# Attention's bulk transfers moved to ScalarE's queue, and a ninth pair of query tiles computed ahead, in a two-layer decoder trunk

## The chip, the core and the metric

The kernel runs on one core of one Trainium2 chip. The metric is device time in microseconds of one execution of the whole program. The kernel before takes 1128.87 us, the median of 3 runs (1127.96 to 1128.97). TensorE is called PE below, VectorE DVE, ScalarE ACT, GpSimd POOL and SyncE SP, as in the profile.

## What is computed

Layer A is a gated linear attention over 1024 tokens of width 1024 with its output projection and a layer norm; layer B, which the change touches, is the second layer:

```python
k, v = shared_kv(x, w_kv)                       # 3 groups x 2 heads x 128, rope on k
q, g = split(x @ w_in)                          # q: 3 groups x 8 heads x 128, rope; g: 8 x 128
for gi, (window, dilation) in enumerate(((128, 1), (512, 4), (2048, 16))):
    o_g, lse_g = dilated_window_attention(q[gi], k[gi], v[gi], window, dilation)
wts = softmax(stack(lses), axis=0)              # weights over the three groups
o = sum(wts * stack(outs))
x = layer_norm(ALPHA * x + (o * silu(g)) @ w_out)
```

All of it is float32. The large products are made of three PE products each (high part by high part, high by low, low by high) in the fast float32r format.

## The kernel before, in words

**Recording and order.** The kernel does not issue instructions itself. It records them with what they read and write into an object `S`, and the scheduler `Sched.order` (line 266) simulates the engines with a table of costs, gives each instruction a planned start, and issues all of them sorted by it. So an edit of one statement, or of a cost, can move instructions on every engine. All instructions therefore carry one source line in the profile (L465), and are told apart by the tiles that they write and read. Each engine then works through its own list strictly in that order; an instruction whose data are late holds up those behind it.

**Transfers.** A `dma_start` is itself an instruction of the engine that issues it: SP issues nearly all, POOL those that add to a tile in flight. The program counts the landing of SP's transfers on eight counters, DMAHW0 to DMAHW7, dealt out in turn in the order of the whole program; a transfer that gets a counter waits until the transfer that had this counter before it has landed. The scheduler's model has one time, `dma_free` (line 293), for all transfers in flight, and does not know the counters.

**Layer B.** It stands in `layer_b` (line 1212) and has three parts.

1. Values, then keys and some queries by pairs. `seven` (line 1295) computes two 1024x128 tiles at once with seven products of half tiles in place of eight (the Strassen-Winograd scheme): 7 products x 4 pieces of depth x 3 = 84 PE instructions of 128x512, tile `sev`. The list `jobs` has three pairs of key tiles, then the pairs of query tiles in `EARLY` (line 41), each entry being two heads and a group: eight pairs, which cover groups 1 and 2 of all eight heads. Results go through the tile `pair` to a DRAM tile `qd`.
2. Attention, one head u after the other (loop at line 1651). `q_proj(u)` (line 1442) gets the three query tiles of a head: those in `qd` are loaded (`Q<-qd`, 512 KB each), the others are computed by `project` (line 687): 2 halves x 8 pieces of depth x 3 = 48 PE instructions of 128x512, tile `acc`. `g_proj(u)` (line 1452) computes the head's gate with another 48. Both take their weights with `load_w` (line 653): a load `wf<-in_wB` of 512 KB, then on ACT the high part `wh<-wf` and a negated copy `wl<-wf`, to which POOL's adding transfer gives the low part. After a query projection ACT copies halves (`t<-acc`) and DVE and POOL rotate them; after a gate projection ACT makes a tanh (`th<-acc`) and DVE the rest (`sg`).
   `scores(u)` (line 1469) makes the score products `lv<-K,Q` on PE; DVE masks each into the tile `P`, with its minimum (`sts`, `nat`), which frees the PSUM bank, of which two are in use; ACT takes the exponential in place. The row statistics are then brought into another order through DRAM with many small transfers: `std<-sts`, `nat<-std`, `cwd<-ew`, `cw<-cwd`, 2 to 4 KB each, 18 per head. `attend(u)` (line 1555) scales P by these weights, transposes it (`ms`), and multiplies with V into two PSUM banks (`po`), from which `og<-po` copies the result. Heads 4 to 7 use a second set of keys and values, so that K and V are loaded again in the middle (`reload_k(1)`, `reload_v(1)`); gated results go to DRAM (`ogB<-og`).
3. The output projection (`ogh`, `ogl` with the weights `in_wOB`) and the layer norm.

All transfers named here are issued by SP but for POOL's adding ones, and land in one ring of SP's.

Of the kernel before, what the change touches and what calls it, by code (L numbers as in the profile page):

```python
# [37 lines left out]
OWN = {"PE": 0.0, "SP": 0.0, "DVE": 0.115, "ACT": 0.11, "POOL": 0.1}  # L38
RUNS, GATHER = 0.3, 1.0
QUEUED, ISSUE, ADDED = 2.4, 0.9, 1.7  # L40
EARLY = [(0, 1, 2), (2, 3, 2), (0, 1, 1), (2, 3, 1), (4, 5, 2), (6, 7, 2), (4, 5, 1), (6, 7, 1)]


class Buf:
# [100 lines left out]
class Sched:  # L145
# [120 lines left out]
    def order(self):  # L266
# [3 lines left out]
        free = {e: 0.0 for e in self.ENG}  # L270
# [19 lines left out]
                for e in o.engs:  # L290
                    ready[e].append(o)
        done = []
        dma_free = 0.0
        cur_set = None
        INF = 1e18

# [32 lines left out]
        while n_done < len(ops):  # L329
            best = None  # L330
            for e in self.ENG:
                cand = None
                for o in ready[e]:
                    if o.t0 is not None:
                        continue
                    r = soft = o.least
                    for d in o.deps:
                        q = ops[d]
                        t = q.t1 + (OWN[e] * (d in o.raw) if q.eng == e else self.pad.get((q.eng, e), self.lat))
                        r = max(r, t)  # L340
                        soft = max(soft, t + (AHEAD if e == "PE" and q.eng in ("ACT", "DVE", "POOL") else 0.0))
                    if o.first:
                        t = alloc_time(o)
                        r = max(r, t)
                        soft = max(soft, t + (AHEAD if e == "PE" and t > 0 else 0.0))
                    if r >= INF:
                        continue
                    k = o.engs.index(e)
                    st = max(free[e], r, port) if o.port[k] else max(free[e], r)
                    if any(max(free[q], r) <= st and c < o.cost[o.engs.index(e)] for q, c in zip(o.engs, o.cost)):  # L350
                        continue

                    key = (max(st, soft), o.prio)
                    if cand is None or key < cand[0]:
                        cand = (key, o, st)
                if cand is not None:
                    (late, pr), o, st = cand
                    if best is None or (late, pr) < best[0]:
                        best = ((late, pr), o, e, st)
            if best is None:  # L360
                left = [o for o in ops if o.t0 is None]
                raise RuntimeError(f"no instruction can be issued; {len(left)} left, first {left[0].calls[0][0]} "
                                   f"{[v.buf.name for v in left[0].writes]}")
            _, o, e, st = best
            c = o.cost[o.engs.index(e)]
            if o.func is not None and e == "ACT":
                new = act_set(o.func, cur_set)
                if new != cur_set:

                    c += 1.3 if cur_set else 0.0  # L370
                    cur_set = new
            o.t0, o.eng = st, e
            if o.calls[0][0] == "dma_start":
                added = e == "POOL"
                dma_free = max(dma_free, st + ISSUE * added) + c * (ADDED if added else 1.0)
                o.t1 = dma_free + (QUEUED if added else 1.7)
                free[e] = st + (ISSUE if added else 0.37)
            else:
                o.t1 = st + c
                free[e] = o.t1  # L380
                if o.port[o.engs.index(e)]:
                    port = o.t1
            for b in o.first:
                if b.placed:
                    continue
                b.placed = True
                tg = tags[id(b.pool), b.tag]
                tg["next"] += 1
                if len(tg["live"]) >= tg["bufs"]:
                    old = min((x for x in tg["live"] if all(u.t0 is not None for u in x.users)),  # L390
                              key=lambda x: max(u.t1 for u in x.users))
                    tg["live"].remove(old)
                tg["live"].append(b)
            for p in {id(v.buf.pool) for v in o.reads + o.writes}:
                pool_users[p]["left"] -= 1
                pool_users[p]["end"] = max(pool_users[p]["end"], o.t1)
            for q in o.engs:
                ready[q].remove(o)
            for s in o.succ:
                s.left -= 1  # L400
                if s.left == 0:
                    for q in s.engs:
                        ready[q].append(s)
            done.append(o)
            n_done += 1
# [216 lines left out]
def trunk(tc, xT, wP, wA, wA12, wAv3, w2, wO, wK, wV0, wV12, wB, wOB, par_d,  # L622
          ident_d, lmask_d, cos_d, sin_d, bmask_d, rmask_d, tri_d, lnr_d, out):
    S = Sched(tc, lat=LAT, pad=PAD)
# [25 lines left out]
        return slice(half * 512, half * 512 + 512)  # L650


    def load_w(src, added=False):
        with S.later(-WEIGHTS):
            return load_w_now(src, added)

    def load_w_now(src, added):
        k, c = src.shape[1], src.shape[2]
        wf = wts.tile([128, 1024], F32, name="wf", bufs=2)
        wf = wf[:, :k * c].rearrange("p (k c) -> p k c", k=k)  # L660
        S.sync.dma_start(wf, src)
        hi = wts.tile([128, 1024], FR, name="wh", bufs=3)
        hi = hi[:, :k * c].rearrange("p (k c) -> p k c", k=k)
        split_hi(hi, wf)
        lo = wts.tile([128, 1024], FR, name="wl", bufs=3)
        lo = lo[:, :k * c].rearrange("p (k c) -> p k c", k=k)
        if added:
            S.scalar.activation(lo, wf, AF.Copy, scale=-1.0)
            S.gpsimd.dma_start(lo, src, accum_op=OP.add)
        else:  # L670
            split_lo(lo, wf, hi)
        return hi, lo
# [515 lines left out]
    kd = [[dram.tile([128, T], F32, name=f"kd{c}{g}") for g in range(3)] for c in range(2)]  # L1188
    vd0 = [dram.tile([128, T], F32, name=f"vd0{c}") for c in range(2)]
# [22 lines left out]
    def layer_b(xs, early):  # L1212
# [27 lines left out]
        K = [[None] * 3 for _ in range(2)]  # L1240
# [139 lines left out]
        def load_v(c, g):  # L1380
            V[c][g] = page(p0, F32, f"V{c}{g}")
            if g == 1:
                for n in range(2):
                    S.sync.dma_start(
                        V[c][g].rearrange("p (r n e) -> p r n e", r=4, n=2)[:, :, n, :],
                        vd[n * 512:n * 512 + 512, c * 128:c * 128 + 128].rearrange("(p r) e -> p r e", r=4))
            else:

                src = vd3[c].rearrange("(n a s k j) e -> k s a n (j e)", n=8, a=8, s=2, k=2)
                for k in range(2):  # L1390
                    for s in range(2):
                        S.sync.dma_start(V[c][g][k * 64:k * 64 + 64, s * 512:s * 512 + 512], src[k, s])

        def sigmoid_gate(sg, acc):
            th = small("th", "t1", 2)
# [21 lines left out]
        def reload_k(c):  # L1417
            for g in (2, 1, 0):
                K[c][g] = page(p0, F32, f"K{c}{g}")
                S.sync.dma_start(K[c][g], kd[c][g])  # L1420

        def reload_v(c):
            load_v(c, 2)
            load_v(c, 1)
            V[c][0] = page(p0, F32, f"V{c}0")
            S.sync.dma_start(V[c][0], vd0[c])

        reload_k(0)

# [12 lines left out]
        def q_proj(u):  # L1442
            Q = [page(p0, F32, "Q") for _ in range(3)]
            U[u]["Q"] = Q
            for g in range(3):
                if (u, g) in qd:
                    S.sync.dma_start(Q[g], qd[u, g])
                else:
                    project(wB[u, g], xs, lambda half, acc: rope(Q[g], g, half, acc), added=u > 0)


        def g_proj(u):
            og = U[u]["og"]

            def evac(half, acc):
                sg, r = small("sg", "t2", 2), hs(half)
                sigmoid_gate(sg, acc)
                S.vector.scalar_tensor_tensor(og[:, r], og[:, r], 0.5, sg, op0=OP.mult, op1=OP.mult)
                if u < 6:
                    S.sync.dma_start(ogB[u][:, r], og[:, r])  # L1460
            project(wB[u, 3], xs, evac, added=True)

        def pieces(P, g, j0):
# [182 lines left out]
            S.vp.memset(x, 0.0)  # L1646
        q_proj(0)
        reload_v(0)
        scores(0)
        q_proj(1)  # L1650
        for u in range(7):
            if u == 3:
                with S.behind(cwd[3]):
                    reload_k(1)
            scores(u + 1)
            if 0 < u < 5:
                g_proj(u - 1)
            if u + 2 < 8:
                q_proj(u + 2)
            attend(u)  # L1660
            if u == 3:
                reload_v(1)
        for u in (4, 5, 6):
            g_proj(u)
        early()
# [185 lines left out]
```

## Time and profile before

| | |
|---|---|
| median of 3 runs | 1128.87 us |
| the profiled execution | 1128.91 us |
| its span, first to last instruction | 1127.1 us |
| granted TensorE clock, mean | 0.999 |
| busy share of the span | PE 99%, PE's weight loads 84%, DVE 73%, ACT 53%, POOL 19% |
| layer A and the values of layer B | 0 to 503 us |
| pairs (`sev`) | 503 to 713 us |
| attention, with the first output products | 713 to 1047 us |
| the rest | 1047 to 1127 us |

A row of the profile names engine, operation, output<-inputs, shape and count, then busy time and the mean duration of one. On PE a matmul of 128x512 stands there with some 390 ns, but the next one starts after 227 ns, because they overlap in the pipeline: a stage's PE time is its number of instructions times their spacing, not the sum of durations. Idle time in square brackets is the gap between the end of one instruction and the start of the next on the engine, with what ended it. On a queue (SPq) a duration is the time in which the sequencer was busy with issuing, not the transfer.

### The profile page before, as it was taken

To read this page: it belongs to the slowest core of one execution; us is meant where nothing else is said; L and a number is where in the kernel's file an instruction comes from. 1 tells how busy PE (TensorE), PEld (TensorE's weight loads), DVE (VectorE), ACT (ScalarE), POOL (GpSimd) and SP (SyncE) were. 2 spreads that over 40 slices of the span, in tenths; PEclk is the share of its full clock that TensorE was granted. 3 is DMA by queue.
4 is the path that set the end of the run, shared out by engine and by line. 5 is a ranking of instruction groups with operands and counts; after the bars stand their busy time and mean duration, and the time that the engine had idled before them with its cause. 6 is when DMAs were issued, how large, how long until landed. Compare 5 with 4: busy or idle time off the path is not lost.

```text
span 1127.1 us, 20068 instructions
## 1 busy us (share of the span) xinstructions
PE 1115.3 (99%) x7648; PEld 950.0 (84%) x7648; DVE 826.0 (73%) x1646; ACT 597.7 (53%) x1199; POOL 214.4 (19%) x209
## 2 busy tenths in 40 slices
PE   9999999999999999999999999999999999999997
PEld 9888888888988888998888888878888888888876
DVE  6286862687968489897888888567875767776578
ACT  5355542546464256666556656476664666643252
POOL 1000100112122031232223232322221123312010
PEclk9999999999999999999999999999999999999999
DMA  7211132221152444865656566955445553442644
GB/s 258 75 39 39 57 95 75 75 76 39 60 191 84 143 163 155 272 193 138 176 133 170 133 175 171 274 111 100 96 111 136 139 127 77 98 120 77 186 134 175
DMA packets 106768, 145.12 MB, mean 129 GB/s; under 512 B 45136, under 2 KB 63440, under 8 KB 106672
## 3 DMA queue, kind: packets, MB, share of 16 engines
q1 hardware_dynamic: 100192, 128.11, 36.5%
q0 software_dynamic: 6480, 15.73, 8.1%
q8 instruction: 60, 0.98, 0.4%
q14 instruction: 36, 0.29, 0.1%
HBM read 112.15 MB, written 31.65 MB: 128 GB/s over the span
## 4 chain that ended last, share of the span: by engine, by line
PE 91%; DVE 4%; DMA 2%; ACT 2%; issue 1%; POOL 0%; SPq 0%; DVEq 0%; ACTq 0%
PE acc L465 42%; PE sev L465 19%; PE po L465 9%; PE lv L465 8%; PE vac L465 7%; PE ms L465 4%; PE pro L465 2%; DMA wf<-in_wOB 1%; DVE P L465 1%; DVE rt L465 1%; DVE wl L465 1%; DVE t L465 0%; DMA xf<-in_xT 0%; DVE x1l L465 0%; ACT t L465 0%
## 5 line engine op out<-in xcount | busy, mean ns | idle before, releaser
L465 ACT ACTIVATE wh<-wf 128x1024 fp32r<-128x1024 f32 (+3 forms) x115 | 105.4, 919 | 159.9 <-PE acc L465 97.3
L465 PE MATMUL acc<-x1h,wh 128*128 128x512 f32 x256 | 114.0, 445 | 0.0
L465 PE MATMUL sev<-T,wh 128*128 128x512 f32 x352 | 108.3, 389 | 0.0
L465 DVE TENSOR_TENSOR wl<-wf,wh 128x1024 fp32r<-128x1024 f32 (+3 forms) x61 | 73.9, 1213 | 42.4 <-ACT wh L465 32.3
L465 PE MATMUL acc<-xh,wh 128*128 128x512 f32 x256 | 101.8, 398 | 0.0
L465 PE MATMUL acc<-x1h,wl 128*128 128x512 f32 x256 | 100.6, 393 | 0.0
L465 PE MATMUL acc<-x1l,wh 128*128 128x512 f32 x256 | 100.1, 391 | 0.0
L465 PE MATMUL acc<-xh,wl 128*128 128x512 f32 x256 | 99.8, 390 | 0.0
L465 PE MATMUL acc<-xl,wh 128*128 128x512 f32 x256 | 99.8, 390 | 0.0
L465 PEld LDWEIGHTS sev<-T,wh 128*128 128x128 f32 x352 | 66.1, 188 | 13.7
L465 ACT ACTIVATE P<-P,sts 128x256 f32<-128x256 f32 (+1 forms) x128 | 59.7, 468 | 30.5 <-DVE sts L465 28.4
L465 POOL DMA_DIRECT2D wl<-in_wB x39 | 34.6, 887 | 209.5 <-ACT wl L465 207.9
L465 PE MATMUL lv<-K,Q 128*64 128x64 f32 (+2 forms) x512 | 71.3, 288 | 1.8 <-DVE sts L465 1.8
L465 PE MATMUL sev<-T,wl 128*128 128x512 f32 x176 | 68.5, 389 | 0.0
L465 PEld LDWEIGHTS lv<-K,Q 128*128 128x128 f32 (+1 forms) x512 | 54.0, 163 | 14.9 <-DVE sts L465 4.4
L465 DVE CUSTOM_DVE_ANT_0 P<-lv,bmask 128x256 f32<-128x256 f32 (+1 forms) x128 | 46.4, 377 | 21.5 <-PE lv L465 21.0
L465 PE MATMUL acc<-ogh,wh 128*128 128x512 f32 x152 | 60.1, 396 | 0.1
L465 PE MATMUL acc<-ogl,wh 128*128 128x512 f32 x152 | 59.3, 390 | 0.0
L465 PE MATMUL acc<-ogh,wl 128*128 128x512 f32 x152 | 59.2, 390 | 0.0
L465 POOL TENSOR_TENSOR wl<-wf,wh 128x1024 fp32r<-128x1024 f32 x10 | 24.2, 2418 | 181.4 <-PE ms L465 91.5
L465 PEld LDWEIGHTS acc<-x1h,wl 128*128 128x128 f32 x256 | 48.0, 188 | 10.8
L465 PEld LDWEIGHTS acc<-xh,wl 128*128 128x128 f32 x256 | 48.1, 188 | 10.3
(304 smaller groups left out, 2997.3 us busy)
## 6 DMA issues: line engine op xcount, KB each, us to landing
wf<-in_wB SPq DMA_DIRECT2D x32, 512.0 KB
wf<-in_wA SPq DMA_DIRECT2D x24, 512.0 KB
wf<-in_wO SPq DMA_DIRECT2D x16, 512.0 KB
qd<-pair SPq DMA_DIRECT2D x16, 512.0 KB
Q<-qd SPq DMA_DIRECT2D x16, 512.0 KB
wf<-in_wOB SPq DMA_DIRECT2D x16, 512.0 KB
wl<-in_wB POOLq DMA_DIRECT2D x15, 512.0 KB, 7.8
wf<-in_wV SPq DMA_DIRECT2D x12, 512.0 KB
```

The lines of the kernel that those rows point to most:

```text
L465: getattr(handle[o.eng], meth)(*[conv(a) for a in args], **{k: conv(v) for k, v in kw.items()})
```

## The change

- `EARLY` gets a ninth pair, (3, 6, 0): group 0 of the heads 3 and 6. `q_proj(3)` and `q_proj(6)` load these two tiles; their two projections fall away.
- A variable `carrier` names the engine that issues the large transfers. It is SP, ACT from behind the first `q_proj(0)` and `reload_v(0)` until the loop over heads has been recorded, then SP again. It holds for weights (`wf`), keys, values, query tiles and gated results. The statistics' transfers always remain on SP.
- The scheduler's model gets one time per queue, and counts 0.6 us for the issue of a small transfer where it counted 0.37.

```diff
-EARLY = [(0, 1, 2), (2, 3, 2), (0, 1, 1), (2, 3, 1), (4, 5, 2), (6, 7, 2), (4, 5, 1), (6, 7, 1)]
+EARLY = [(0, 1, 2), (2, 3, 2), (0, 1, 1), (2, 3, 1), (4, 5, 2), (6, 7, 2), (4, 5, 1), (6, 7, 1),
+         (3, 6, 0)]
...
-        dma_free = 0.0
+        queues = {"SP": 0.0, "ACT": 0.0, "POOL": 0.0}
...
-                dma_free = max(dma_free, st + ISSUE * added) + c * (ADDED if added else 1.0)
-                o.t1 = dma_free + (QUEUED if added else 1.7)
-                free[e] = st + (ISSUE if added else 0.37)
+                line = "ACT" if e == "ACT" else "SP"
+                queues[line] = max(queues[line], st + ISSUE * added) + c * (ADDED if added else 1.0)
+                o.t1 = queues[line] + (QUEUED if added else 1.7)
+                small = max(int(_np.prod(v.shape)) for v in o.reads[:1] + o.writes[:1]) <= 2048
+                free[e] = st + (ISSUE if added else 0.6 if small else 0.37)
...
+    carrier = [S.sync]
+
...
-        S.sync.dma_start(wf, src)
+        carrier[0].dma_start(wf, src)
...
-                S.sync.dma_start(K[c][g], kd[c][g])
+                carrier[0].dma_start(K[c][g], kd[c][g])
...
-                    S.sync.dma_start(Q[g], qd[u, g])
+                    carrier[0].dma_start(Q[g], qd[u, g])
...
-                    S.sync.dma_start(ogB[u][:, r], og[:, r])
+                    carrier[0].dma_start(ogB[u][:, r], og[:, r])
...
         q_proj(0)
         reload_v(0)
+        carrier[0] = S.scalar
         scores(0)
...
             if u == 3:
                 reload_v(1)
+        carrier[0] = S.sync
         for u in (4, 5, 6):
```

The four transfers of `load_v` and the last one of `reload_v` are changed in the same way.

In the program as built, PE has 1008 instructions `sev` where it had 924, and 672 of 128x512 with x1 into `acc` where it had 768. ACT issues 43 transfers: 16 `Q`, 9 `wf`, 8 `ogB`, 7 `V` and 3 `K`. SP keeps those of head 0, the weights of the last four gates, and the statistics. Up to the eighth query pair every engine's list is unchanged.

**ACT, early in attention.** Before, the first heads' weights, query copies (`t`) and the exponentials of head 0 stand there like this:

```order
L465 ACTIVATE t_7128<-acc 64x512 x2
L465 ACTIVATE wh<-wf 128x1024
L465 ACTIVATE wl<-wf 128x1024
L465 ACTIVATE t_7188<-acc 64x512 x2
L465 ACTIVATE t_7217<-acc 64x512 x2
L465 ACTIVATE P,nat<-P,nat 128x64 x8
L465 ACTIVATE P,sts<-P,sts 128x128
```

The same place after the change:

```order
L468 ACTIVATE wh<-wf 128x1024
L468 ACTIVATE wl<-wf 128x1024
L468 DMA wf<-in_wB 128x1024
L468 ACTIVATE t_7363<-acc 64x512 x2
L468 ACTIVATE P,nat<-P,nat 128x64 x4
L468 ACTIVATE t_7420<-acc 64x512 x2
L468 ACTIVATE P,nat<-P,nat 128x64 x4
```

The load of the next weights now stands on ACT between the negated copy that frees its tile and the query copies that DVE waits for. In six of the nine such places a `t` or `th` stands right behind the load.

**SP before, ACT after, at the second set of values.** The rows are shown with what they wait for (DMAHW0 to DMAHW7 are the counters, the others engines; `std` and `nat` are statistics of head 4). Before, on SP:

```order
L465 DMA std_8745<-sts 128x2x4 [waits DMAHW3_49,Activation_49]
L465 DMA Q<-qd_6972 128x1024 [waits DMAHW4_49,PE_49]
L465 DMA Q<-qd_6644 128x1024 [waits DMAHW5_49]
L465 DMA V_8810<-vd_4625 64x1x512 [waits DMAHW6_49,PE_49]
L465 DMA V_8810<-vd_4625 64x1x512 [waits DMAHW7_49]
L465 DMA V_8824<-vd 128x4x128 [waits PE_49]
L465 DMA V_8847<-vd_4834 128x1024 [waits DMAHW1_49,PE_49]
L465 DMA std_8745<-sts 8x16x8 [waits DMAHW2_49,DVE_49]
```

After, on ACT:

```order
L468 DMA Q<-qd_6982 128x1024 [waits DMAHW0_49]
L468 DMA Q<-qd_6644 128x1024 [waits DMAHW4_49]
L468 DMA V_8933<-vd_4625 64x1x512 [waits DMAHW5_49,Pool_49]
L468 ACTIVATE P,sts<-P,sts 128x256 [waits DVE_49] x2
L468 DMA V_8933<-vd_4625 64x1x512 [waits DMAHW6_49]
L468 DMA V_8944<-vd 128x4x128 [waits DMAHW7_49,PE_49]
L468 DMA V_8951<-vd_4834 128x1024 [waits DMAHW0_49,PE_49]
L468 ACTIVATE og<-po 128x64x4 x2
L468 ACTIVATE P,sts<-P,sts 128x256 [waits DVE_49] x2
L468 DMA V_8933<-vd_4625 64x1x512 [waits DMAHW1_49]
```

Seven value transfers and two query loads now stand between ACT's exponentials and its copies out of the `po` banks. The counters are dealt out over both queues together, so `V_8951`, which gets DMAHW0 after `Q<-qd_6982`, waits on ACT until that load has landed.

More of the change, by code (lines that the diff above doesn't have):

```diff
@@ L1383, in load_v @@
                 for n in range(2):
-                    S.sync.dma_start(
+                    carrier[0].dma_start(
                         V[c][g].rearrange("p (r n e) -> p r n e", r=4, n=2)[:, :, n, :],
@@ L1391, in load_v @@
                     for s in range(2):
-                        S.sync.dma_start(V[c][g][k * 64:k * 64 + 64, s * 512:s * 512 + 512], src[k, s])
+                        carrier[0].dma_start(V[c][g][k * 64:k * 64 + 64, s * 512:s * 512 + 512], src[k, s])
         def sigmoid_gate(sg, acc):
@@ L1425, in reload_v @@
             V[c][0] = page(p0, F32, f"V{c}0")
-            S.sync.dma_start(V[c][0], vd0[c])
+            carrier[0].dma_start(V[c][0], vd0[c])
         reload_k(0)
```

## The prediction

> **What bounds the kernel now.** I read the page first, then busy time by stage, then the spacing of PE's instructions, then the places where PE sits idle in the stage that changes.
>
> ```profile
> span 1127.1 us, 20068 instructions
> PE 1115.3 (99%) x7648; PEld 950.0 (84%) x7648; DVE 826.0 (73%) x1646; ACT 597.7 (53%) x1199; POOL 214.4 (19%) x209
> ```
>
> ```profile
> core 0: us, PE busy (x) PEld busy (x) DVE busy (x) ACT busy (x) POOL busy (x), PEclk, DMA share, GB/s
> ...
> 503.30:712.76 209.46, 209.46 (x925) 173.42 (x925) 170.11 (x247) 126.87 (x218) 58.68 (x57) 1.00 0.61 162
> 712.76:1046.60 333.84, 332.05 (x2074) 286.45 (x2073) 235.11 (x776) 191.62 (x582) 78.30 (x103) 1.00 0.49 119
> ```
>
> The rows of the second view are the stage of the pairs and attention. PE is never idle in the first and idle for 333.84 - 332.05 = 1.79 us in the second, at the full granted clock (1.00). A busy PE need not be a PE at its pace, so I take the spacing from the chain of work that ended last, whose rows are start, time, instruction and count:
>
> ```profile
> 503.30 209.47 PE sev L465 x924
> 712.76 17.00 PE acc L465 x75
> ```
>
> 209.47 / 924 = 0.2267 us, and 17.00 / 75 = 0.2267 us: the products of the pairs and those of the ordinary projections cost PE the same, each 128x512, and the eleven pairs go through without a gap. So PE's list is the bound in both stages, and a change is worth what it takes off that list plus or minus what PE waits. The waits of attention are few. The timeline of PE shows them; the first two rows are how each looks, the others are the late instruction alone:
>
> ```profile
> 741.54 0.40 PE L465 MATMUL acc<-x1h,wl 128*128 128x512 f32 x1
> 742.30 0.38 PE L465 MATMUL lv<-K,Q 128*128 128x128 f32 x1 [0.37 <-DVE sts L465]
> ...
> 760.31 0.48 PE L465 MATMUL lv<-K,Q 128*128 128x256 f32 x1 [0.46 <-DVE sts L465]
> ...
> 796.01 0.38 PE L465 MATMUL lv<-K,Q 128*128 128x128 f32 x1 [0.20 <-DVE sts L465]
> ...
> 884.12 0.48 PE L465 MATMUL lv<-K,Q 128*128 128x256 f32 x1 [0.60 <-DVE sts L465]
> ...
> 979.81 0.48 PE L465 MATMUL lv<-K,Q 128*128 128x256 f32 x1 [0.15 <-DVE sts L465]
> ```
>
> Each is a score product that waits for a PSUM bank which DVE has yet to read. The gaps sum to 1.78 us, all of the stage's idle time. What is lost is a little more, since the product ahead lasts 0.40 us where the next would start after 0.23: 5 x 0.17 = 0.85 more, 2.6 us in all. That is the most that better timing in attention can bring, and no transfer stands as the releaser of any of the five.
>
> **The ninth pair.** Removed from attention are two projections of 2 x 8 x 3 = 48 PE instructions, 96 x 0.2267 = 21.76 us; added to the pairs are 7 x 4 x 3 = 84, 19.04 us. PE's list gets shorter by 12 x 0.2267 = **2.72 us**. The new pair's other work lies beside PE: by the stage's row a pair costs DVE 170.11 / 11 = 15.5 us, ACT 11.5 and POOL 5.3 against PE's 19.04. If that cover failed there would be a gap after a pair, and there is none in eleven. Its two stores and two loads of 512 KB are new, 2 MB in a stage whose transfer engines are busy for 0.61 and another with 0.49; I count them at nothing, and at 0.3 us at most, half of the largest gap above, should one delay a page.
>
> In attention the projections also leave the other engines:
>
> ```profile
> L465 ACT ACTIVATE wh<-wf 128x1024 fp32r<-128x1024 f32 x19 | 20.1, 1060 | 32.0 <-PE acc L465 23.2 <-PE lv L465 4.4 <-PE po L465 4.4
> L465 ACT ACTIVATE t<-acc 64x512 f32<-64x512 f32 x32 | 19.0, 593 | 12.7 <-DVE t L465 9.9 <-PE acc L465 2.5
> L465 ACT ACTIVATE wl<-wf 128x1024 fp32r<-128x1024 f32 x13 | 13.5, 1042 | 0.0
> ```
>
> ACT loses 2 x (1.06 + 1.04 + 4 x 0.593) = 8.9 us, so 191.6 becomes 182.7.
>
> **ACT as an issuer.** No trace here has ACT issuing a transfer; the nearest rows are those of the same transfers on SP (shortest, middle, longest ns on the queue):
>
> ```profile
> L465 SPq DMA_DIRECT2D Q<-qd x16: 377/440/974, 720.1 to 950.9; - x16
> L465 SPq DMA_DIRECT2D wf<-in_wB x32: 328/333/732, 536.0 to 922.2; - x32
> L465 SPq DMA_DIRECT2D V<-vd x14: 321/572/751, 721.3 to 891.8; - x14
> L465 SPq DMA_DIRECT2D ogB<-og x12: 320/325/1135, 788.8 to 999.5; - x12
> L465 SPq DMA_DIRECT2D K<-kd x6: 319/374/448, 697.2 to 860.5; - x6
> ```
>
> 16 x 0.440 + 9 x 0.333 + 7 x 0.572 + 8 x 0.325 + 3 x 0.374 = 17.8 us. ACT then has 182.7 + 17.8 = 200.5 us of work in a stage of 333.8 - 21.8 = 312 us, 64% in place of 57%. So ACT does not become the bound, and the price is only what falls into a wait of PE. Here the chain of waits shows the path, in the piece ahead of the first late score product and at two others:
>
> ```profile
> 737.50 1.04 ACT wl L465
> ...
> 738.56 0.59 ACT t L465
> ...
> 739.16 0.60 ACT t L465
> ...
> 739.79 1.92 DVE t L465
> ...
> 742.30 1.04 PE lv L465 x4
> ...
> 755.84 1.04 ACT wl L465
> ...
> 973.69 1.04 ACT wl L465
> ```
>
> Three of the five late products hang on a `wl`, then a `t` or `th`, then DVE. After the change a weight load stands between the two in six of nine cases. Three of the stage's thirteen `wl` had a late product behind them; so I count 6 x 3/13 x 0.333 = **0.46 us**. The bounds: 6 x 0.333 = 2.0 us if each is uncovered; below, a gain of the 2.6 us above if the new order happens to close all the gaps. I lie near the low end because the three rows that show the path are the nearest evidence.
>
> The Trainium skill, page "Perfetto Trace Analysis", section "Sequencer Loop", says that a sequencer pushes an engine's instructions into a queue and itself executes only control instructions. By that an issue would hold back what stands behind it while ACT works off what was pushed, and my 0.46 would shrink towards nothing, the sum to the bare 2.72. The rows of SP cannot show it, since SP has no such work; I leave the 0.46.
>
> SP loses the same 43 issues. What that frees is the statistics: they no longer queue behind 512 KB in one ring. I count no gain, since none of the five waits names them, and PE has nothing to do sooner.
>
> **The sum.** 1128.91 (profiled execution) - 2.72 + 0.46 = 1126.65, with the median 0.04 below that execution: **1126.6 us**. 0.2% is 2.26 us, about what a measurement here can tell from no change, and 1128.87 - 2.26 = 1126.61. The forecast sits on that edge.
>
> **Rivals.** *Thinner cover: no change.* With 21.8 us fewer filler products for the same scores, the five gaps could double.
>
> ```profile
> 780.00:820.00 40.00, 39.80 (x287) 35.35 (x285) 31.94 (x123) 23.96 (x89) 9.18 (x13) 1.00 0.40 80
> ...
> L465 DVE TENSOR_TENSOR t<-t,sinT 128x512 f32<-128x512 f32 x14 | 12.3, 876 | 9.1 <-ACT t L465 9.0
> ...
> L465 DVE TENSOR_TENSOR t<-acc,cosT 128x512 f32<-128x512 f32 x16 | 11.1, 691 | 11.4 <-PE acc L465 7.7 <-ACT t L465 3.7
> ...
> L465 DVE TENSOR_TENSOR Q<-t,t 128x512 f32<-128x512 f32 x8 | 5.8, 720 | 0.1
> ```
>
> In this stretch, where one of the two projections runs, DVE (third number with a count) is busy for 31.9 of 40 us. Without it PE has 40 - 10.9 = 29.1 us, and DVE 31.9 - 2 x (0.69 + 0.88 + 0.72) = 27.3, which is 94% of it. That speaks for it; against it, the gates of heads 4 to 6 are bound to no place and can be drawn forward. 2.6 us more of waiting gives 1128.87 - 2.72 + 2.6 = 1128.8 us. Beside it stands a rule: the Trainium skill, page "DMA: Bandwidth & Descriptors", section "Issuing engines are not separate DMA queues", says that transfers of all issuers run on the same 16 engines and interleave, and that more issuers save only the sequencer's time. By it the second queue would take nothing off PE's waits either.
>
> *The gaps close: faster.* If the new order meets DVE better, 2.72 + 2.6 are gained: 1123.6 us. For it: the five gaps are accidents of order, not a lack of capacity. Against it: nothing in the change aims at DVE.
>
> *ACT held at a counter: slower.* ACT now waits in its own list until an earlier transfer has landed. The second set of values shows it best: `V_8951` waits for the counter of `Q<-qd_6982`, with only four issues between. Issuing those five takes 2 x 0.440 + 3 x 0.572 = 2.6 us. What 512 KB take from issue to release the chain shows for output weights:
>
> ```profile
> 1054.71 3.70 DMA wf<-in_wOB
> ...
> 1061.28 4.77 DMA wf<-in_wOB
> ...
> 1068.42 6.43 DMA wf<-in_wOB
> ```
>
> So ACT stands still for 3.70 - 2.6 = 1.1 us up to 3.8. Behind it are the copies `og<-po` that free PE's two banks for the next value products, and exponentials that DVE and the transposes need. A second such wait follows (the last `V`, behind the first). Two waits at 3.8 us that PE cannot cover cost 7.6 us: 1128.87 - 2.72 + 7.6 = 1133.8. It decides from 2.72 + 2.26 = 5.0 us of PE idle, below that it only eats the gain. Against it: SP stood in such waits before and ACT has 112 us to spare in the stage, and PE has transposes and scores between one head's value products.
>
> *The change does not do what it says* in small part: the weights of the last four gates stay on SP between the statistics. That moves no time that I counted.
>
> **How the numbers follow.** Forecast 0.50, with its own range of 1125.6 to 1127.6, a little more than half of it below the edge, as there is more room under 0.46 for hidden issues than evidence above; thinner cover 0.22; gaps close 0.15; ACT held 0.13. Faster by over 0.2%: 0.15 + 0.30 = 0.45. Within 0.2%: 0.20 + 0.22 = 0.42. Slower: 0.13. The range takes the forecast, thinner cover with one more microsecond, and most of the closing gaps: 1124.0 to 1129.8; left out are most of ACT held and the end of the other side, under 0.2.
>
> **What would show it.** In the profile after: the chain should have some 1008 products `sev` in 228.5 us without a gap, and attention should take 312 us and what PE idles. PE's idle time there says which case it is: about 2 us with the same releaser (DVE sts) is the forecast, 4 and over is thinner cover, near 0 is the third. ACT held would show as PE waiting for ACT `og` or for `acc` banks around the second set of values, with ACT idle behind its own transfers. I am wrong if PE's idle in attention moves by more than 2 us, if the pairs' stage shows gaps, or if the spacing of PE's products changes.

## The result, and the profile after

The changed kernel is slower: 1140.59 us median (1138.12 to 1144.44, 4 runs) beside 1128.66 us before (1127.96 to 1128.97, 4 runs), a ratio of 1.011 with a 95% interval of 1.0075 to 1.0144. Its runs spread over 6.3 us where those of before spread over 1.0. The profiled execution is the slowest of them, 1144.44 us with a span of 1142.3 us, so its trace shows the loss at its upper end: 15.2 us of span.

The page of the changed kernel, its first rows and the two rows of the slices that matter:

```profile
span 1142.3 us, 20057 instructions
PE 1119.4 (98%) x7636; PEld 954.0 (84%) x7636; DVE 834.9 (73%) x1655; ACT 599.0 (52%) x1202; POOL 217.1 (19%) x219
...
PE   9999999999999999999999999999998899999997
...
PEclk9999999999999999999999999999999799999999
```

PE has its 12 products less, and still more busy time (1119.4 against 1115.3 us). The last row says why that can be: in the 32nd of the 40 slices, 885 to 914 us, the granted clock is 0.7. Busy time by stage, the stages cut as in the prediction; the end of the second is set where the third group of 24 output products begins, 1062.53 us here and 1046.65 us before:

```profile
503.74:732.25 228.51, 228.51 (x1010) 189.25 (x1009) 186.47 (x271) 138.03 (x237) 62.35 (x61) 1.00 0.61 162
732.25:1062.53 330.28, 316.94 (x1977) 274.43 (x1977) 227.04 (x761) 182.03 (x566) 77.31 (x109) 0.97 0.48 117
```

The same view of the kernel before, with that end:

```profile
712.76:1046.65 333.89, 332.10 (x2074) 286.51 (x2073) 235.11 (x776) 191.67 (x582) 78.30 (x103) 1.00 0.49 119
```

The pairs behave as forecast: 19.05 us more, no gap. Attention should have become 21.76 us shorter and became 3.61 us shorter. PE idles 330.28 - 316.94 = 13.34 us in it in place of 1.79, which is 11.55 of the 18.15 us that are missing; the other 6.6 us lie in products that run while the granted clock is low. An estimate from the trace agrees: the clock stood at half for three stretches of attention in which PE was busy for 13.87 us (they are shown at the end), and half of that is 6.9 us. With 0.44 us ahead of the pairs and -0.68 behind attention the span closes: 0.44 + 19.05 - 3.61 - 0.68 = 15.2.

What PE waited for in attention (engine and line waited for: us in total, times, longest):

```profile
PE lv L468 <- DVE nat L468: 5.5, 1, 5.5
PE lv L468 <- DVE sts L468: 3.3, 3, 2.8
PE po L468 <- DVE og L468: 2.3, 1, 2.3
PE po L468 <- ACT og L468: 1.6, 1, 1.6
```

Three places, with four waits, make nearly all of it, where before had five gaps of 0.15 to 0.60 us. **The first** is read from the chain of waits (start, time, what):

```profile
868.11 1.71 DMA cwd<-ew
...
870.01 10.85 DMA cw<-cwd
...
881.31 1.20 ACT P L468 x3
...
886.91 0.77 PE lv L468 x2
```

`cw`, the coefficients of head 3 (two transfers of 4 KB), is the last step of its statistics, and the first of the two takes 10.85 us to land. SP issued that one at 870.01, and ACT the three reloads of K at 870.33, into its own queue. Before, the same transfers went out on one queue, and DVE worked with the coefficients 2.2 us after the first of their two transfers was issued (the first rows are SP's timeline, the last is DVE's):

```profile
857.55 0.37 SPq L465 DMA_DIRECT2D cw<-cwd  x1
...
859.03 0.37 SPq L465 DMA_DIRECT2D cw<-cwd  x1
859.50 1.40 SPq L465 DMA_DIRECT2D K<-kd  x3
```

```profile
859.73 2.72 DVE L465 TENSOR_SCALAR P<-P,cw 128x128 f32<-128x128 f32 x11 [1.19 <-DMA cw<-cwd]
```

The queues of the changed kernel between 872 and 876 us show what goes on (queue: packets, MB, share of 16 engines; q1 is SP's, q10 is ACT's, which the kernel before does not have):

```profile
q10 hardware_dynamic: 333, 1.23, 92.1%
q1 hardware_dynamic: 202, 0.00, 2.8%
```

The engines that move data give 92.1% of their time to K's large packets, and the small packets of `cw`, issued earlier, get through at 202 in 4 us. ACT's and DVE's lists have work on these coefficients ahead of the instructions that empty the banks for head 4's scores, so PE waits for a bank.

**The second place** (903 to 909 us, two waits) is the rival "ACT held at a counter", as it was described: ACT stands still for 3.64 us ahead of an exponential, behind its own reload of V, and the copies `og<-po` that PE needs come late.

```profile
900.09 0.19 ACT L468 ACTIVATION_READ_ACCUMULATOR P<-P,sts 128x1 f32 x1
902.44 1.42 ACTq L468 DMA_DIRECT2D V<-vd  x1
903.91 0.51 ACT L468 ACTIVATE P<-P,sts 128x256 f32<-128x256 f32 x1 [3.64 <-issue]
```

The counter that V waits for belongs to a statistics write, `std<-sts`, issued at 895.57 and landed 6.80 us later. ACT then stands a second time, for another 3.64 us:

```profile
908.64 0.38 ACT L468 ACTIVATE og<-po 128x256 f32<-128x256 f32 x1 [3.64 <-PE ms L468]
```

Ahead of this copy stand two more reloads of V. The first of them was issued at 907.33, when a `nat<-std` with the same counter had landed at 907.26, and its issue ended only behind PE's transposes (`ms`), which the row names. **The third** (963 us, 2.8 us) comes from a DVE instruction that lasts 3.94 us in place of 0.41; it is taken up at the end.

Each of these waits costs more than its length. Behind the first one, PE's timeline reads:

```profile
886.91 0.77 PE L468 MATMUL lv<-K,Q 128*128 128x128 f32 x2 [5.52 <-DVE nat L468]
887.32 0.77 PE L468 MATMUL acc<-x1h,wh 128*128 128x512 f32 x1
887.90 0.63 PE L468 MATMUL acc<-x1l,wh 128*128 128x512 f32 x1
888.32 0.63 PE L468 MATMUL acc<-x1h,wl 128*128 128x512 f32 x1
```

The products start 0.42 us apart in place of 0.23, for 5 us.

### The profile page after: what moved, and what is told of

It is laid out like the page before. It is cut to its first block, busy times and chain, and to the rows that moved or that the text cites. A ratio compares the mean times of both kernels' runs of the same rounds, so it can differ in the third digit from the quotient of the medians.

```text
span 1142.3 us, 20057 instructions
## 1 busy us (share of the span) xinstructions
PE 1119.4 (98%) x7636; PEld 954.0 (84%) x7636; DVE 834.9 (73%) x1655; ACT 599.0 (52%) x1202; POOL 217.1 (19%) x219
## 4 chain that ended last, share of the span: by engine, by line
PE 88%; DMA 4%; DVE 4%; ACT 2%; issue 1%; ACTq 0%; SPq 0%; DVEq 0%
PE acc L468 38%; PE sev L468 20%; PE po L468 9%; PE lv L468 8%; PE vac L468 7%; PE ms L468 4%; PE pro L468 2%; DMA std<-sts 1%; DMA cw<-cwd 1%; DVE P L468 1%; DVE rt L468 1%; DVE lnA L468 1%; ACT t L468 1%; DMA V<-vd 0%; DMA wf<-in_wOB 0%
## 5 line engine op out<-in xcount | busy, mean ns | idle before, releaser
L468 PE MATMUL sev<-T,wh 128*128 128x512 f32 x384 | 118.3, 389 | 0.0
L468 PE MATMUL acc<-x1h,wh 128*128 128x512 f32 x224 | 102.1, 456 | 0.0
L468 PE MATMUL acc<-x1h,wl 128*128 128x512 f32 x224 | 89.1, 398 | 0.0
L468 PE MATMUL acc<-x1l,wh 128*128 128x512 f32 x224 | 88.5, 395 | 0.0
L468 PEld LDWEIGHTS sev<-T,wh 128*128 128x128 f32 x384 | 72.1, 188 | 15.0
L468 PE MATMUL lv<-K,Q 128*64 128x64 f32 (+2 forms) x512 | 74.2, 292 | 9.5 <-DVE nat L468 5.5
L468 PE MATMUL sev<-T,wl 128*128 128x512 f32 x192 | 74.7, 389 | 0.0
L468 PEld LDWEIGHTS po<-PT,V 128*128 128x128 f32 x432 | 54.1, 196 | 6.5 <-issue 2.5
L468 PE MATMUL po<-PT,V 128*128 128x128 f32 x432 | 55.6, 281 | 3.9 <-DVE og L468 2.3
```

The costliest lines, as they stand in the source:

```text
L468: getattr(handle[o.eng], meth)(*[conv(a) for a in args], **{k: conv(v) for k, v in kw.items()})
```

## The experiments

All times are medians, each beside runs of the kernel before on the same chip (1128.1 to 1128.5 us).

**First theory: the second queue starves the statistics (ring theory).** Rivals: ACT standing at counters (counter theory); and cover theory, by which the two projections that the pair takes away had been what PE did while a head's statistics were under way. The pair alone:

```diff
-EARLY = [..., (4, 5, 1), (6, 7, 1)]
+EARLY = [..., (4, 5, 1), (6, 7, 1), (3, 6, 0)]
```

> The kernel before with the ninth pair alone; all transfers stay on SP and the planner's model of the queues is the old one. Ring theory (a small statistics transfer on SP's ring is starved while bulk runs on ACT's ring) and counter theory (ACT stands still at a landing counter): the pair is innocent, 12 products of 0.2267 us go, 1126.1 us, between 1124.5 and 1128. Cover theory (21.8 us fewer filler products leave the scores uncovered): the loss stays, 1135 us or more, with several us of PE idle in attention.

Measured: 1134.13 us, ratio 1.0054 (1.0042 to 1.0066). The pair, with nothing else changed, loses 6.0 us. Neither 1126 nor quite 1135 and more: the pair is not innocent, as cover theory said, with a little less loss. The main wait is at 943 us; chain of waits:

```profile
943.41 0.02 ACT wh L466
...
944.37 1.04 ACT wl L466
945.41 2.19 ACT P L466 x6
```

The coefficients had landed at 942.2, but ACT's list has the next weights ahead of the probabilities, and these are made only when PE has finished with the last ones.

The rest of the change without the pair:

```diff
-EARLY = [..., (4, 5, 1), (6, 7, 1), (3, 6, 0)]
+EARLY = [..., (4, 5, 1), (6, 7, 1)]
```

> The changed kernel with eight pairs instead of nine: bulk on ACT's queue, new model of the queues. Ring and counter theory: still slower than before, by 5 to 15 us, 1134 to 1144 us, with statistics transfers of 6 us and more next to bulk on the other ring. Cover theory: within 2 us of 1128.9.

Measured: 1138.99 us, 1.0093 (1.0071 to 1.0116). So the rest loses nearly as much without the pair, and the two losses do not add up (6.0 and 10.9, together 11.9).

Then the order of the changed kernel, kept on every engine, with single transfers issued elsewhere. K on SP:

```diff
+eng = "SP" if meth == "dma_start" and o.eng == "ACT" and o.writes[0].buf.name.startswith("K1") else o.eng
-getattr(handle[o.eng], meth)(...)
+getattr(handle[eng], meth)(...)
```

> The changed kernel's plan and every engine's order untouched, but the three reloads of K for heads 4 to 7 are issued on SP, behind the two small transfers that feed the coefficients. Ring theory: those two land in about 2.3 us instead of 10.8 and 8.2, the 5.5 us wait of PE at 881 us goes, and with it the half-clock stretch behind it (12 products, 2.8 us): 7 to 8 us less than the changed kernel, about 1132.5 us. Counter theory and cover theory: ACT's waits and the products are as before, so within 2 us of the changed kernel, 1140.6.

Measured: 1141.01 us, 1.0108 (1.0095 to 1.0121). The ring theory falls as the whole cause of the loss. What it says of `cw` came true: no `cw` transfer of attention takes more than 3.7 us from issue to landing now, and the 5.5 us wait is gone. But K comes behind it, and K is needed just then (what PE waited for, two of the rows):

```profile
PE lv L469 <- DMA ogB<-og: 2.0, 1, 2.0
PE lv L469 <- DMA K<-kd: 0.9, 1, 0.9
```

Both are products of head 4's scores, at 882 us (the 2.0 us) and at 877 us. The view names `ogB` for the one at 882 us, which landed in the same tenth of a microsecond; the second reload of K, which that product reads, was issued at 872.38 and landed 9.4 us later by its counter, at 881.8. The other waits, of 2.9, 2.7 and 1.7 us, are those of the second and third place again. Of coefficients and K one has to be second, and this order leaves room for neither. All 43 transfers on SP:

```diff
+eng = "SP" if meth == "dma_start" and o.eng == "ACT" else o.eng
```

> The changed kernel's plan untouched, but all 43 bulk transfers are issued on SP in the plan's order; ACT issues none. Ring theory: the small transfers issued ahead of bulk are safe again, those behind it wait as in the kernel before; counter theory: ACT's stand at 900 us (3.6 us) goes too. Both: 1126 to 1132 us. Cover theory, or a plan that is bad by itself: 1138 us or more.

Measured: 1138.04 us, 1.0083 (1.0066 to 1.01). ACT is held nowhere and issues nothing, and still 9.9 of the 11.9 us are lost: most of the loss is in the order.

**Second theory: the order is the fault.** The opposite experiment keeps the order of before and only issues the 43 transfers on ACT:

```diff
+eng = "ACT" if isinstance(o.engs, Bulk) else o.eng      # Bulk: the 43 transfers, planned as SP's
```

> The kernel before, its plan and the order on every engine untouched (eight pairs, old model of the queues); only the 43 bulk transfers of attention are issued by ACT on its own queue. Cover theory (what is lost is the projections that stood between scores, statistics and value products) and plan theory (the order made for two independent queues is the fault): issuing by itself costs little, within 2 us of 1128.3. Issuer theory (ACT standing at counters, or two rings sharing the 16 engines, is the fault): 1132 us or more, with PE waiting for ACT or for statistics that land late.

Measured: 1130.23 us, 1.0015 (1.0006 to 1.0024): 1.8 us. And the order of the new model with eight pairs, issued by SP:

> Eight pairs and the order that the new model of two queues makes, but every transfer issued on SP: the kernel before in everything but the order. Plan theory: slower by 4 us or more, 1132 to 1139 us, as when ACT issued them in this order (1139.0). Issuer theory: within 2 us of 1128.3. Cover theory: within 2 us of 1128.3 too, since all projections are there.

Measured: 1139.86 us, 1.01 (1.0082 to 1.0119): eight pairs, no issue on ACT, and the whole loss. In the profiled execution, the fastest of the five (1136.24 us), one wait makes nearly all of it, and SP's timeline shows its origin:

```profile
PE ms L468 <- DVE cw L468: 7.4, 1, 7.4
```

```profile
880.00 1.22 SPq L468 DMA_DIRECT2D V<-vd  x2
881.27 4.50 SPq L468 DMA_DIRECT2D nat<-std  x4
885.88 1.15 SPq L468 DMA_DIRECT2D wf<-in_wB  x1
887.07 2.20 SPq L468 DMA_DIRECT2D V<-vd  x3
```

The loads `nat` of head 4's statistics stand among Q, V and weights, and land 7.3 to 8.9 us after their issue. That the new model put them there because it reckoned bulk on a line of its own is tested next.

The model has two edits. The new 0.6 us for issuing a small transfer taken back:

```diff
-free[e] = st + (ISSUE if added else 0.6 if small else 0.37)
+free[e] = st + (ISSUE if added else 0.37)
```

> Eight pairs, all transfers on SP, the order made with two independent lines but with the old 0.37 us for issuing a small transfer. Optimism theory: the two lines are the fault (2.9 us reckoned for a statistics transfer), so 1135 to 1143 us as with both edits (1139.9). If the 0.6 us is the fault: within 2 us of 1128.4.

Measured: 1139.26 us, 1.0098 (1.0085 to 1.0111). Then the two lines as well:

```diff
-line = "ACT" if e == "ACT" else "SP"
+line = "SP"
```

> Differs from the run with two lines and 0.37 us (1139.3 us) in one line of the model: the transfers of both issuers are reckoned on one shared line. Eight pairs, all issued on SP. Theory of the shared line (the engines that move data are one, so an order is good only if it was made for one line): 1128 to 1132 us. Rival (any order made anew loses): 1135 us or more.

Measured: 1128.25 us, 1.0 (0.9992 to 1.0009). These two runs differ in this one line and by 11.0 us. It is a new order too, and loses nothing; its longest wait of PE is

```profile
PE ms L468 <- DVE PT L468: 1.3, 1, 1.3
```

The same order with ACT really issuing:

> The order of the run with one shared line and eight pairs (1128.3 us with all transfers on SP), now with the 43 bulk transfers really issued by ACT. Theory of the shared line: ACT as issuer costs little once the order reckons with one line, as it cost 1.8 us on the order of before: 1128 to 1131 us. If ACT as issuer has a loss of its own: 1133 us or more.

Measured: 1128.36 us, 1.0001 (0.9992 to 1.001). ACT as an issuer costs nothing that can be measured, in an order that reckons with one line.

**How the two lines hurt.** A margin for small transfers in the model with two lines, eight pairs, SP issuing:

```diff
+o.t1 += 1.2 if small else 0.0
```

> As the run with eight pairs, the new model's order and all transfers on SP (1139.9 us), and one term added to the model: a small transfer is reckoned to land 1.2 us later. The planner then reckons 4.3 us for a statistics transfer on average in attention, where the old model reckoned 4.1, the new one 2.8, and the trace of before showed 3.3; its schedule still leaves PE no gap. Optimism theory (the new model reckons the statistics to land sooner than they do, and puts their users too early in each engine's list): 1128 to 1131 us. Rival (any order made anew loses against the one before, which is a lucky one; or two lines are bad for another reason): 1136 us or more.

Measured: 1133.87 us, 1.0048 (1.0036 to 1.006), between the theories: about half comes back. What is left is mainly a wait of 3.0 us for K and one of 1.1 us; K's time was still reckoned on its own line. The same margin in the changed kernel:

> The changed kernel, ACT issuing, nine pairs, with the 1.2 us added for a small transfer in the model. Optimism theory: the losses at heads 3 to 5 go, and what is left is what the planner itself then leaves open, 5 us more than for the kernel before, nearly all in one gap at head 7 after 1015 us: 1131 to 1135 us. Rival (ACT as issuer, or any new order, is the fault): 1138 us or more.

Measured: 1141.22 us, 1.012 (1.0102 to 1.0138): a miss, nothing came back. A `cw` takes 11.34 us, now at another head, beside bulk on ACT's and POOL's queues (chain of waits):

```profile
930.10 11.34 DMA cw<-cwd
```

But that cost PE only 1.3 us. PE's two longest waits there, 3.2 and 3.6 us of 10.3 in all, stand behind no late transfer but behind DVE copies that lasted 4.57 and 3.46 us while POOL worked beside them, as at the third place of the changed kernel. The second of them, and what POOL did:

```profile
960.34 3.46 DVE L469 COPY_PREDICATED P<-above,P 128x128 f32<-128x128 uint8 x1 [0.86 <-ACT P L469]
```

```profile
960.83 2.80 POOL L469 TENSOR_TENSOR Q<-t,t 128x512 f32<-128x512 f32 x2
```

So this run does not decide whether the statistics were reckoned too short: the 5.5 us wait of PE is not there, and other waits took its place. Moving V alone, in the order that lost 11 us:

```diff
+late = [o for o in done if ... o.writes[0].buf.name.startswith("V1")]
+done = [o for o in done if o not in late]
+done[k:k] = late             # k: behind the last load of head 4's statistics
```

> The order of the run with eight pairs, the new model and all transfers on SP (1139.9 us; PE waits 7.4 us at 886 us for a chain through loads of statistics that land in 7.3 to 8.9 us), with one edit after planning: the seven transfers that reload V for heads 4 to 7 are issued behind the last load of head 4's statistics in place of among them. Theory of the shared line: those loads land in about 3 us, and the wait of PE shrinks by 4 us or more: 1130 to 1136 us. If bulk is not what delays them: within 2 us of 1139.9.

Measured: 1136.14 us, 1.0076 (1.0054 to 1.0098). The wait shrinks from 7.4 to 4.7 us. The four loads that had taken 7.3 to 8.9 us landed in 3.8 to 5.8 us. That is 2.7 us less waiting where 4 or more was expected, and the time, at the upper end of what was expected, has an interval that overlaps that of the order untouched. V is part of the delay by the wait, less surely by the time; whether Q and the weights, which stay, are the rest was not tried.

**The pair and the cover.** Two other pairs, the old model, SP alone:

```diff
-         (3, 6, 0)]
+         (2, 6, 0)]      # and, in the other run, (5, 6, 0)
```

> The ninth pair made of heads 2 and 6 in place of 3 and 6; old model, all transfers on SP. The products removed and added are the same in number; only the heads that lose their projection differ. Cover theory: the loss goes by place. The planner's own schedule leaves PE 4.5 us more than before with (3, 6), which measured 6.0 us more than before; with (2, 6) it leaves 1.8 us more: 1129 to 1132 us. A cost that goes with the pair itself (more transfers among the pairs, one more store): 1134 us, as (3, 6).

> The ninth pair made of heads 5 and 6, two heads that follow each other; old model, all transfers on SP. Cover theory: both heads in a row lose their filler, the planner's schedule leaves PE 13 us more than before, nearly all in one gap of 9 us; 1137 to 1144 us, with one PE wait of 6 us or more at head 6. A cost that goes with the pair itself: 1134 us, as (3, 6).

Measured: 1129.92 us, 1.0013 (1.0004 to 1.0022), and 1140.9 us, 1.0118 (1.0102 to 1.0133). The same number of products moved, the same transfers added, and 1.5, 6.0 or 12.4 us lost by which heads give their projection: cover theory, by place. Each pair also makes a newly planned order, so the times alone do not separate the two; that the planner's own schedules had left PE 1.8, 4.5 and 13 us more, in the same order as the losses, speaks for the cover. For (5, 6), what PE waited for:

```profile
PE ms L466 <- ACT P L466: 8.1, 1, 8.1
PE lv L466 <- DVE sts L466: 2.6, 7, 0.5
```

Now the chain itself made shorter, with nine pairs. This kernel leaves out writing the coefficients to DRAM and reading them back, so it scales the probabilities with other numbers and does not compute the reference; `reload_k(1)` then follows the coefficients themselves:

```diff
-for g in range(2): ... S.sync.dma_start(cwd[u][g]..., ew[...])     # 4 per head
-S.sync.dma_start(cw[:, 0:8], ...); S.sync.dma_start(cw[:, 8:16], ...)
```

> Nine pairs, old model, all transfers on SP, and the last two of the four transfer steps of each head's statistics left out (48 small transfers: the coefficients are not written out and read back, so the probabilities are scaled with other numbers). Cover theory (without 21.8 us of products the chain of statistics is longer than what PE has to do beside it): the planner's schedule has no gap, and the pair gives its full 2.7 us: 1125 to 1127 us. Rival (the pair costs by itself, or attention waits for something else): 1131 us or more, near the 1134.1 of the pair alone.

Measured: 1122.25 us, 0.995 (0.9938 to 0.9962), 2.8 us below the expected stretch: without the two steps even before's five gaps close. The prediction's own terms give the time: 1128.13 - 2.72 for the pair - 2.6 for the gaps is 1122.8 us. So with the chain short the pair brings what was forecast of it. What PE waited for:

```profile
PE lv L466 <- DVE sts L466: 0.3, 1, 0.3
```

The same two steps left out of the changed kernel:

> The changed kernel, nine pairs, ACT issuing, two lines in the model, with the last two transfer steps of each head's statistics left out (48 small transfers; the probabilities are scaled with other numbers), as in the run that gave 1122.3 us with the old model and SP alone. If the late statistics are all that the changed kernel loses: 1121 to 1126 us. If ACT as issuer or the loads of K, Q and V are a loss of their own: 1129 us or more.

Measured: 1126.66 us, 0.9988 (0.9979 to 0.9996), 0.7 us above the expected stretch. 14 us of the changed kernel go with two short transfer steps per head; 4.4 us stay against the run above; how they divide between the two queues and the order was not taken apart.

Last, the changed kernel with one shared line and 0.37 us:

> The changed kernel (nine pairs, ACT issuing) with the transfers of both issuers reckoned on one shared line and 0.37 us for every issue on SP. The planner's schedule then leaves PE 11 us more than with eight pairs, in many gaps after heads 3 to 6, of which the pair gives 2.7 back. Cover theory: 1134 to 1139 us, the pair still a loss. If two lines were all that is wrong with the change: 1126 to 1129 us.

Measured: 1144.62 us, 1.0145 (1.0123 to 1.0166), above what cover theory gave. The pair stays a loss when the model is put right: 16.3 us against the same kernel with eight pairs (1128.36 us), the sum of many waits, none over 1.9 us, and of a clock that fell three times:

```profile
PE ms L468 <- ACT P L468: 3.8, 3, 1.7
PE lv L468 <- DVE sts L468: 2.4, 6, 0.9
PE po L468 <- ACT diag L468: 1.9, 1, 1.9
```

The runs that compute the whole reference, side by side:

| pairs | lines in the model | issued by SP | issued by ACT |
|---|---|---|---|
| 8 | one | 1128.66 (before), 1128.25 | 1130.23, 1128.36 |
| 8 | two | 1139.86, 1139.26 | 1138.99 |
| 9, (3, 6) | one | 1134.13 | 1144.62 |
| 9, (3, 6) | two | 1138.04 | 1140.59 (the change) |

In the rows of one line, 1128.66, 1130.23 and 1134.13 us were planned with SP as the issuer, 1128.25, 1128.36 and 1144.62 us with ACT. None of them beat the kernel before by more than the noise.

## Why the prediction was wrong

It forecast 1126.6 us and gave "slower" 0.13. Of its own signs of being wrong, one came: PE's idle time in attention moved by 11.55 us, where it allowed 2. Two of its steps failed, the price of the pair and the model that it gave no term. By its own steps:

- **What bounds the kernel:** right. PE's list is the bound, and the pairs' stage went as forecast, 1008 products in 228.51 us:

```profile
503.74 228.51 PE sev L468 x1008
```

- **The ninth pair, -2.72 us:** this step failed. The sum itself was right, and was collected where the chain of statistics had been cut short. But it priced what leaves PE's list and then asked only whether the new pair's side work is covered among the pairs. It did not ask what the two projections had been covering in attention: each head has four transfers in a row between its scores and its value products, and a projection of 10.9 us is what PE does meanwhile. The rival *thinner cover* had the mechanism with the wrong size and the wrong engine: it doubled five DVE gaps (2.6 us). Measured alone, the pair is a loss of 6.0 us net, so 8.7 us of new waits and low clock. That price belongs to the order of before: in the changed kernel the pair adds 1.6 us, which is within the noise (1140.59 against 1138.99 us), and with one line and ACT reckoned as issuer 16.3 us.
- **The model of the queues:** no term at all. The prediction weighed who issues the transfers and gave nothing to the edit that reckons them on two lines, though that edit decides where every instruction of attention stands. It is worth 11.0 us by itself, so it carries most of the loss of 11.9 us. The sentence "what that frees is the statistics" took over the model's belief; at head 3 the coefficients took 10.85 us where they had taken 2.2. The rule that stood beside the rival, from the Trainium skill, page "DMA: Bandwidth & Descriptors", section "Issuing engines are not separate DMA queues" (all issuers' transfers run on the same 16 engines), was used only against a gain. What follows from it for a planner is not on the page: a plan that reckons with two independent queues counts the same 16 engines twice. The runs fit that: 1139.26 us with two lines, 1128.25 us with one.
- **ACT as an issuer, +0.46 us:** small, as forecast. On the order of before it cost 1.8 us (0.7 to 2.7 by the interval), more than 0.46 and inside the bound of 2.0; on the order for one line nothing. The changed kernel's trace also shows an issue that held up no work: the third load of K was issued at 871.49, while ACT worked on `wl` from 871.05 to 872.09.
- **ACT held at a counter:** it happened where it was described, twice in a row, 3.64 us each time for ACT and 3.9 us together for PE. Both counters belonged to small statistics transfers, not to the load of Q that the rival named, and the second stand ended behind PE. The length per stand was within its 1.1 to 3.8 us; it is not what made the result, since without any issue on ACT the order still takes 1138.0 us.
- **What a wait costs:** the sums took a wait at its length. Here waits of 13.3 us came with 6.6 us of slow products behind them.

What stays open: which transfers put beside each other make the 11.0 us of the two lines (moving V behind the statistics took 2.7 of the 7.4 us of the wait away); how the 11.9 us of the whole change divide. The pair alone costs 6.0 and the order alone 10.9 to 11.4; each opens waits in places that the other has opened already. Why the pair with one line and ACT reckoned as issuer (1144.6 us) is worse than with the old model and SP (1134.1 us) was not taken apart.

## What to carry to other kernels

When filler work is moved away from a stage, price what it had been hiding, head by head: the latency of the chain that ran beside it against the work that is left. When a planner's model is edited, the order it makes is the change. Here a second issuing queue by itself changed nothing that could be measured (1128.36 against 1128.25 us), while a model with two independent lines put 2 KB loads that everything waits for among transfers of up to 512 KB (1139.26 us). Test the model and the issuer apart, with the same order issued both ways.

## What the runs showed of the hardware

- **A small transfer that is issued first can be overtaken by a large one on another queue.** 4 KB that landed in 2.2 us with K behind it on one queue (issued at 859.03, K from 859.50) took 10.85 us with K on the other; with K put back on SP's queue, behind it, at most 3.7 us. The Trainium skill, page "DMA: Bandwidth & Descriptors", section "Queues, rings and completion order", says that each engine goes round-robin between the queues at packet granularity; the 202 small packets beside 333 large ones in 4 us fit that, though not one for one.
- **The granted clock changes in steps of 3.41 us, and falls behind waits of 2 us as well as 5.** The three low stretches of the changed kernel's attention (busy time by window; the granted clock is the third number from the end):

```profile
885.40:892.20 6.80, 5.29 (x15) 4.39 (x16) 2.96 (x27) 4.79 (x24) 0.00 (x0) 0.50 0.00 0
905.90:912.70 6.80, 5.17 (x21) 4.60 (x22) 2.61 (x10) 2.23 (x8) 0.77 (x2) 0.50 0.49 154
967.30:970.70 3.40, 3.40 (x10) 2.63 (x9) 1.72 (x9) 1.84 (x7) 0.12 (x1) 0.51 0.88 305
```

  The waits were 5.5 us; 2.3, then 1.6 us; and 2.8 us. The stretches last two, two and one time 3.41 us, and they start 20.5 and 61.4 us after one another, 6 and 18 times 3.41: the trace shows changes of the clock on such a grid only. Length alone does not decide it. In the changed kernel with the margin the clock stayed at 1.00 behind a wait of 3.2 us:

```profile
907.20:913.00 5.80, 5.63 (x27) 4.51 (x28) 5.59 (x18) 3.69 (x12) 0.00 (x0) 1.00 0.68 211
```

  That wait lies across the edge of two steps, by the same grid 1.4 us in one and 1.9 us in the next. The three steps at whose end the clock of the changed kernel fell had 3.4, 2.3 and 2.4 us of idle PE. Over attention in all traces of this case, it fell only behind steps with 1.7 us or more, about half a step, and it did not fall behind any step with more than 1.9 us.

- **DVE can stand still beside POOL.** A predicated copy that takes 0.41 us on average in the kernel before lasted 3.94 us while POOL worked on SBUF, and made the 2.8 us wait of PE at 963 us (DVE's row, then POOL's):

```profile
961.52 3.94 DVE L468 COPY_PREDICATED P<-above,P 128x128 f32<-128x128 uint8 x1 [0.26 <-ACT P L468]
```

```profile
961.81 2.85 POOL L468 TENSOR_TENSOR Q<-t,t 128x512 f32<-128x512 f32 x2
```

The kernel before has one such copy too (3.00 us at 880.53), ahead of the longest of its five gaps. The Trainium skill, page "GPSIMD Engine Reference", section "Specifications", lists SBUF interfaces shared with VectorE, with contention for DVE instructions that have two SBUF inputs; the copy has two, the mask and `P`. The same copy lasted 3.5 to 4.6 us beside POOL's work, with a PE wait of 2.4 to 3.6 us behind it, in three more kernels with nine pairs and the model of two lines: K on SP (3.95 us), all on SP (3.50 us), and with the margin, twice. That POOL is the cause was read from such rows and not tried.
